# Layer 0's output projection in a two-layer streaming trunk: finished channels read back during the third head pair, and the value store in two parts

## The chip, the cores and the metric

The kernel runs on one core of a Trainium2 chip. The time is that of one execution on the device in microseconds, the median of the runs. Everything is kept feature-major: 128 features on the partitions, tokens along the columns. There are 1152 token columns, 1024 of a prompt and 8 x 16 of running streams, handled in three groups of 384 (G).

## The reference

Two layers, each a mixer and a squared-ReLU MLP with residuals and norms. The change is in the mixer of layer 0, which runs stick-breaking attention (8 heads of 64) beside a convolution module (512 channels, 31 taps), and joins both in one output projection:

```python
def ab_mixer_prompt(h, w_in, w_out, dw_w, dw_b, ln_g, ln_b):
    q, k, v, u = ab_project(h, w_in)             # u = a * sigmoid(g)
    ...
    a_out = a_out.reshape(B, T, SB_WIDTH)        # stick_breaking(q, k, v) over blocks of queries
    u_ext = jnp.pad(u, ((0, 0), (CONV_STATE, 0), (0, 0)))
    c_out = conv_module(u_ext, dw_w, dw_b, ln_g, ln_b)   # depthwise conv, layernorm, silu
    out = jnp.concatenate([a_out, c_out], axis=-1) @ w_out
    return out, k, v, u[:, T - CONV_STATE:]
```

The same is done for the running streams, whose keys and values come from a cache of 1024 positions. k and v are outputs too. The joined input of the projection has eight chunks of 128 features: chunks 0 to 3 are the attention's head pairs, chunks 4 to 7 the convolution's channels.

## The kernel before, in words

`mixer0` (L676) goes through four head pairs (`for p in range(4)`, L1004). Each large product is made of three passes over a high and a low part of the operands, so whatever TensorE multiplies with weights must first be split: ScalarE copies the high part (`split`, L186), VectorE subtracts it (L187). `put` issues a DMA from POOL's queue, `dma` one from SyncE's (SP in the profile). DMAs of either queue are issued in order, and an issue that has to wait holds what stands behind it.

**A pair.** `proj(p)` projects q, k and v of pair p in three groups of columns each; groups 0 and 1 are written by VectorE (L898), group 2 by ScalarE (L900). Once group 2 of k or v is there, POOL stores the whole tile (`sk`, `sv`) as an output (L902). `expand_qk` then splits q and k (L367, L369, L370, L372). `differences` (L914) replaces v in place by differences of neighbouring positions (L922 on VectorE, the first column L923 on ScalarE); since it overwrites `sv`, it has to wait until the store of L902 has read it. `expand_v` (L925) transposes the result (`vt`, L932). `attend` computes scores (`z`, L962, L963, L965), sigmoids (L966) and scans (L942, L947, L948), transposes the weights (`tpa`, L407), multiplies with the values (`ava`, L417) and sums the pieces (`cpa`, L431). Pairs 0 to 2 put their finished pieces in DRAM (`cat_d`, L382); pair 3 splits them straight into its place. The streams' attention (`zs`, `sgs`, `kps`; L589, L990 to L995) runs in between with cached keys (`ct03k`, loaded by SyncE, L558).

**The convolution.** Four channels groups c = 0 to 3 of 31 taps each (`tap`, L756) run on VectorE as filler: 26 taps beside the first projection, then 36, 38 and 24 in pairs 0, 1 and 2 (`TAPS`). The tiles `u` (input, two buffers, so channel 2 takes channel 0's place) and `y` lie in a pool `conv`. After the last tap POOL stores the result to `cat_d` (L759, L760).

**The last pair.** Pairs 0 to 2 have the next pair's projection as filler on TensorE; pair 3 has the output projection instead (`part_out`): for each output chunk of 128 features, sums over the read-back chunks 0 to 2 (`psoa`, L226). Its first three sums, over chunks 0 and 1 only, stand at its start (`first`). `ready_chunks` reads a chunk back from `cat_d` into the single buffer of the tag "sk" (`cr`, SyncE, L1100) and splits it into `cat0`. In the order of the work, chunks 0 and 1 are read back ahead of `first`, chunk 2 later (named "ready", 3 us of estimated work behind the last pieces of pair 2). `xo` (L1132) are the residual's rows, loaded by SyncE for each output chunk. Beside that, `conv_norm` (L1039) closes the pool `conv`, opens a pool `ln` in its place, loads the four channels of a column group (`yl`, L1053, POOL), takes the mean on TensorE (`mu`, L1059), centres (L1061), sums the squares (`ms_l`, L265), makes the reciprocal root on VectorE and ScalarE and broadcasts it by a product with diagonals (`rr_l`, L287).

**What sets the order.** `merge` interleaves lists of steps by an estimated TensorE time, respecting "after" and "lag"; `level` spreads the taps; the framework's scheduler then orders each engine's instructions, and each engine works through its own in order. The pool `early0` (`ep`) holds three buffers of the tag "sg" and two of "kp", which the streams' `kps` use (L987).

Of the kernel before, what the change touches and what calls it, by code (L numbers as in the profile page):

```python
# [8 lines left out]
F32 = mybir.dt.float32  # L9
# [6 lines left out]
P = 128  # L16
D = 1024
KC = 8
T = 1152
TP = 1024  # L20
TAPS = (26, 36, 38, 24)
G = 384
NG = 3
# [8 lines left out]
UW = UP + 8 * US  # L32
# [92 lines left out]
def tile_trunk(ctx, tc, ins, outs):  # L125
# [6 lines left out]
    put = nc.gpsimd.dma_start  # L132
# [43 lines left out]
    cat_d = [dram.tile([KC, P, T], F32, name=f"cat_d{l}") for l in range(2)]  # L176
# [7 lines left out]
    def split(hi, lo, src):  # L184

        ACT(hi, src, AF.Copy)  # L186
        return tt(lo, src, f(hi), ALU.subtract)  # L187
# [488 lines left out]
    def mixer0():  # L676
        with ExitStack() as st:

            ep = Bufs(st.enter_context(pool("early0")), sg=3, kp=2)
# [6 lines left out]
            pp = Bufs(st.enter_context(pool("pair0")), ve=2)  # L686
            wk = Bufs(st.enter_context(pool("work0")), wt=4, wts=1, cat=2)
            S = {"qb": qb}
# [15 lines left out]
            h, rstd = n0.h, n0.r  # L704


            us, ys, tapped = {}, {}, [0] * 4
            conv_pool = ExitStack()
            cv = Bufs(conv_pool.enter_context(pool("conv")), u=2, y=1)

# [30 lines left out]
            def tap(c, j):  # L741
                if j == 0:
                    ys[c] = cv.tile([P, T], F32, "y", f"y{c}")
                u, y = us[c], ys[c]
                wj = dw[:, c, j:j + 1]
                pairs = ((y[:, 0:TP], u[:, j:j + TP]),
                         (y[:, TP:].rearrange("p (b t) -> p b t", t=16),
                          u[:, UP:].rearrange("p (b t) -> p b t", t=US)[:, :, j:j + 16]))

                with tc.issue_after(prior["weights"].ins) if prior else ExitStack():  # L750
                    for dst, src in pairs:
                        if j == 0:
                            nc.vector.tensor_scalar(dst, src, wj, cvec[:, 0, c:c + 1], ALU.mult, ALU.add)
                        else:

                            stt(src if j == CW - 1 else dst, src, wj, dst, ALU.mult, ALU.add)  # L756
                tapped[c] += 1
                if j == CW - 1:
                    put(cat_d[0][4 + c, :, 0:TP], pairs[0][1])  # L759
                    put(cat_d[0][4 + c, :, TP:].rearrange("p (b t) -> p b t", t=16), pairs[1][1])  # L760
# [130 lines left out]
            def proj(p):  # L891
                steps = []
                for n, tag in enumerate(("sq", "sk", "sv")):
                    def evac(ps, g, n=n, tag=tag):
                        if g == 0:
                            S[tag, p] = pp.tile([P, T], F32, tag, f"{tag}0{p}")
                        if g < 2:
                            tt(S[tag, p][:, g * G:g * G + G], ps[:, :G], rstd[g], ALU.mult)  # L898
                        else:
                            ACT(S[tag, p][:, g * G:], ps[:, :G], AF.Copy)  # L900
                        if g == 2 and n:
                            put(outs["sb_k" if n == 1 else "sb_v"][p], S[tag, p])  # L902
                    steps += chunk_steps(at[4 * n + p], got, ahead, h, ks, evac, f"p{p}{n}")
                return steps

# [98 lines left out]
            for p in range(4):  # L1004
                S["p"] = p
                expand_qk(p)
                if p < 3:
                    fill = proj(p + 1)
                    if p < 2:
                        fill[10:10] = ag(p + 2)  # L1010
                    n = TAPS[p + 1]
                    mix, now, taps = [], taps[:n], taps[n:]
                else:
                    cat_t = new_hs("cat0")
                    (first, fill), now = part_out(0, range(3), pp, cat_t), []
                    for s in taps:
                        s.pe = 900.0
                    mix = taps + conv_norm(lambda: (conv_pool.close(), Bufs(st.enter_context(pool("ln")), t1=3, yl=5))[1],
                                           cat_t)
                cat = Cat(0, p, wk, cat_t)  # L1020
                jobs = attend(p, cat)
                body, left = pipeline(jobs[1:], jobs[0][2])
                steps = carry + [jobs[0][0]] + [Step(327.0, lambda p=p, g=g: expand_v(p, g)) for g in range(NG)]
                if p == 3:
                    late, = ready_chunks(0, [2], pp, cat_t)
                    late.name, late.after, late.lag = "ready", carry[-1].name, 3000.0
                    fill[0].after, fill[0].lag = "ready", 5000.0
                    fill = ready_chunks(0, range(2), pp, cat_t) + first + [late] + fill
                steps += [jobs[0][1]] + body
                carry = left  # L1030
                if p == 3:
                    steps += carry
                cs = sample_out(cat, wk, p)
                load = sample_caches(0, p, cp)
                sample = two_samples(*(sample_steps(0, p, bg, S, wk, load, soft, cs) for bg in range(2)))
                run(level(merge(steps, sample, fill, mix), now))
# [1175 lines left out]
```

## Time and profile before

| what | value |
|---|---|
| median of 3 runs | 2701.9 us (2701.33 to 2704.93) |
| the profiled execution's own time | 2699.14 us |
| its span | 2697.4 us |
| granted TensorE clock, mean | 0.995 |
| instructions | 42135 |
| HBM read, written | 299.56 MB, 122.58 MB |
| pair 0's value store issued | 104.85 us |
| the last pair's first read-back issued | 399.43 us |

The profile is of one execution; its times count from the start of the span. A row of the timeline has start, duration, engine, line, operation, output<-input, number of instructions, and in brackets how long the engine was idle before it and what released it. Tile names come without their numbers. PE is TensorE, PEld its weight loads, DVE VectorE, ACT ScalarE, POOL GpSimd, SPq SyncE's DMA queue.

### The profile page before, as it was taken

The page shows a single profiled execution, that of the slowest core. Times are in us where ns is not written, and L with a number is a line of the kernel's source. Part 1 is how long each engine was busy: PE and PEld are TensorE (multiplying, and loading weights), DVE is VectorE, ACT ScalarE, POOL GpSimd, SP SyncE. Part 2 cuts the span into 40 slices and gives each one's busy share as a digit, 9 for nine tenths or more (in the row PEclk, how much of TensorE's full clock was granted, in tenths as well). Part 3 has the DMA queues.
Part 4 walks back from the last instruction along what each step waited for, and adds up shares of the span by engine and source line. Part 5 has one row for each costly group of instructions (what it writes and reads, how often), then busy time and mean ns, then how long its engine had stood idle before and what let it go on. Part 6 is the DMA issues. An engine that isn't in the chain of part 4 may idle for free.

```text
span 2697.4 us, 42135 instructions
## 1 busy us (share of the span) xinstructions
PE 2643.2 (98%) x15404; PEld 2313.8 (86%) x15404; DVE 1989.0 (74%) x3820; ACT 1344.6 (50%) x2691; POOL 315.4 (12%) x535
## 2 busy tenths in 40 slices
PE   8999998999999999999999999999999999999998
PEld 8888886888888878888999999989988888888888
DVE  8999996896767654768577777778786767546677
ACT  6344456754444543445355555556554545433444
POOL 1100111131111100000011111110311111100001
PEclk9999999999999999999999999999999999999999
DMA  4344547534444497435444444446534444685344
GB/s 160 110 126 150 152 143 240 177 126 145 149 148 147 160 311 247 142 116 194 152 142 134 136 142 135 136 140 231 185 120 144 155 148 148 252 289 170 99 148 141
DMA packets 194095, 437.56 MB, mean 162 GB/s; under 512 B 26992, under 2 KB 71216, under 8 KB 191840
## 3 DMA queue, kind: packets, MB, share of 16 engines
q1 hardware_dynamic: 154320, 298.22, 33.9%
q0 software_dynamic: 39424, 136.64, 14.3%
q8 instruction: 121, 1.98, 0.3%
q14 instruction: 86, 0.70, 0.1%
q10 hardware_dynamic: 144, 0.02, 0.0%
HBM read 299.56 MB, written 122.58 MB: 156 GB/s over the span
## 4 chain that ended last, share of the span: by engine, by line
PE 83%; DVE 8%; issue 3%; ACT 3%; DMA 2%; POOL 0%; SPq 0%; DVEq 0%; ACTq 0%; POOLq 0%
PE um L1606 22%; PE psc L226 10%; PE psp L226 4%; PE usm L1618 3%; PE ps L1909 3%; PE psoa L226 2%; PE avc L488 2%; PE tpc L476 2%; PE f L226 1%; PE pd103None L1889 1%; PE pd100None L1889 1%; PE pd003None L1889 1%; PE pd000None L1889 1%; PE pd001None L1889 1%; PE pd101None L1889 1%
## 5 line engine op out<-in xcount | busy, mean ns | idle before, releaser
L226 PE MATMUL psc<-h,hl_wc 128*128 128x384 f32 x1728 | 328.8, 340 | 0.0
L226 PEld LDWEIGHTS psc<-h,hl_wc 128*128 128x128 f32 x1728 | 296.8, 188 | 9.2 <-issue 7.9
L1606 PE MATMUL um<-sl,hl_m 128*128 128x512 f32 x780 | 197.2, 393 | 0.0
L756 DVE SCALAR_TENSOR_TENSOR y<-u,dw,y 128x1024 f32<-128x1024 f32 (+1 forms) x232 | 177.7, 807 | 0.7
L1606 PEld LDWEIGHTS um<-sl,hl_m 128*128 128x128 f32 x780 | 145.1, 188 | 30.2
L226 PE MATMUL psp<-h,hl_wi 128*128 128x384 f32 x864 | 162.4, 340 | 0.0
L187 DVE TENSOR_TENSOR tm<-xr,tm 128x512 fp32r<-128x512 f32 (+1 forms) x120 | 78.6, 657 | 108.0 <-ACT tm L186 107.9
L226 PEld LDWEIGHTS psp<-h,hl_wi 128*128 128x128 f32 x864 | 148.3, 188 | 6.2 <-issue 5.1
L186 ACT ACTIVATE tm<-xr 128x512 fp32r<-128x512 f32 (+1 forms) x120 | 72.1, 600 | 118.7 <-PE pd103None L1889 21.3
L1230 ACT ACTIVATE s<-s,mxc 128x640 f32<-128x640 f32 (+4 forms) x128 | 88.8, 693 | 40.2 <-DVE mxc L1227 38.5
L186 ACT ACTIVATE whc<-tpc 128x512 fp32r<-128x512 f32 (+1 forms) x144 | 72.4, 524 | 63.7 <-PE tpc L476 60.4
L1227 DVE CUSTOM_DVE_ANT_0 s<-zc,bp 128x384 f32<-128x384 f32 (+3 forms) x128 | 66.1, 517 | 41.2 <-PE zc L1264 40.6
L1606 PE MATMUL um<-sl,hl 128*128 128x512 f32 x372 | 95.0, 395 | 0.0
L187 DVE TENSOR_TENSOR wlc<-tpc,whc 128x512 fp32r<-128x512 f32 (+1 forms) x144 | 83.2, 594 | 7.6 <-ACT whc L186 7.0
L1606 PEld LDWEIGHTS um<-sl,hl 128*128 128x128 f32 x372 | 70.0, 190 | 14.3
L1630 ACT ACTIVATE xr<-xr 128x512 f32<-128x512 f32 x64 | 40.4, 631 | 80.8 <-DVE xr L1629 80.8
L476 PE MATMUL tpc<-ident,s 128*128 128x128 f32 x480 | 73.6, 276 | 2.6 <-DVE s L1232 2.1
L187 DVE TENSOR_TENSOR xr<-xr,xr 128x512 fp32r<-128x512 f32 (+1 forms) x60 | 39.4, 656 | 46.9 <-ACT xr L186 46.9
L187 DVE TENSOR_TENSOR th<-xr,th 128x512 fp32r<-128x512 f32 (+1 forms) x62 | 40.8, 658 | 42.1 <-ACT th L186 42.1
L186 ACT ACTIVATE hl_m<-xr 128x512 fp32r<-128x512 f32 x54 | 34.1, 632 | 74.6 <-PE usm L1618 61.4
L186 ACT ACTIVATE th<-xr 128x512 fp32r<-128x512 f32 (+1 forms) x62 | 37.3, 601 | 66.4 <-PE pd003None L1889 13.1
L1263 PE MATMUL zc<-k,q 128*128 128x384 f32 (+1 forms) x192 | 66.2, 346 | 2.9 <-DVE cpc L498 2.9
(1050 smaller groups left out, 7166.4 us busy)
## 6 DMA issues: line engine op xcount, KB each, us to landing
xr<-hb_d SPq DMA_DIRECT2D x208, 256.0 KB, 2.8
xr<-in_w_up_dram SPq DMA_DIRECT2D x32, 512.0 KB, 3.7
rwm<-in_w_up_dram SPq DMA_DIRECT2D x32, 512.0 KB, 5.0
hb_d<-xr POOLq DMA_DIRECT2D x32, 512.0 KB, 3.4
hb_d<-t POOLq DMA_DIRECT2D x32, 512.0 KB, 3.2
wm<-in_w_down_dram SPq DMA_DIRECT2D x64, 256.0 KB, 3.4
st_wd<-in_w_down_dram SPq DMA_DIRECT2D x64, 256.0 KB, 3.5
st_wc<-in_w_in_c_dram SPq DMA_DIRECT2D x44, 256.0 KB, 2.9
```

The source lines that it names most:

```text
L186: ACT(hi, src, AF.Copy)
L187: return tt(lo, src, f(hi), ALU.subtract)
L226: mm(ps()[:, :G], hl[:, a, at:at + P], act[g][k // 4][b][:, k % 4, :], start=n == 0, stop=n == len(todo) - 1)
L476: nc.tensor.transpose(tp[:, c0 + q * P:c0 + (q + 1) * P], blocks.get(j, tile_q), ident)
L756: stt(src if j == CW - 1 else dst, src, wj, dst, ALU.mult, ALU.add)
L1227: nc.vector.tensor_tensor_reduce(s[:, c:c + m], z, b, -1.0, mx, ALU.add, ALU.min, new)
L1230: ACT(s[:, :n], s[:, :n], AF.Exp, bias=mx, scale=-1.0, accum_out=tot)
L1263: mm(z[:, :m], qs[i][:, qc], kd[i][:, kc], start=True, stop=False)
L1606: mm(banks[b, e], w[a][:, c], combo(key, c)[:, h], start=k < 3 and c == 0 and i == 0, stop=c == 3 and i == 2, skip_group_check=k > 2)
L1618: mm(samples[u][:, e * 256:e * 256 + 256], sample_combo(key, c)[h], w[a][:, c].rearrange("p e t -> p (e t)"), start=k == 0 and c == 0 and ...
L1889: mm(ps, w[:, a, m * P:m * P + P], b[:, h], start=first and s == 0, stop=j == NJ - 1 and s == 2, skip_group_check=k not in heads)
L1909: mm(rows[e], s[:, h], w[:, a], start=j == 0 and q == 0 and k != 0, stop=j == NJ - 1 and q == 2 and k != 3, skip_group_check=k in (3, 0))
```

## The change

Two things.

1. At tap 20 of channel 3, the 14th of the 24 taps in pair 2, POOL issues two reads: chunk 1 into a buffer `cr1` of the tag "kp" (a streams' buffer), and chunk 0 into `cr0` of the tag "u" (the place of channel 2, whose taps are over). The splits of both become six steps of their own at pair 3's start: four, then two steps carried over from pair 2, then the last two. `ready_chunks(0, range(2))` goes from the head of the filler; chunk 2 is read back as before.
2. The value store is split by columns: 0 to 767 once group 1 is written, 768 to 1151 once group 2 is. The store of k stays whole.

```diff
@@ mixer0
-            us, ys, tapped = {}, {}, [0] * 4
+            us, ys, tapped, crs = {}, {}, [0] * 4, {}
...
@@ tap(c, j)
                 tapped[c] += 1
+                if (c, j) == (3, 20):
+                    crs[0] = cv.tile([P, UW], F32, "u", "cr0")
+                    crs[1] = ep.tile([P, T], F32, "kp", "cr1")
+                    for n in (1, 0):
+                        put(crs[n][:, :T], cat_d[0][n])
                 if j == CW - 1:
...
@@ proj(p), evac
-                        if g == 2 and n:
-                            put(outs["sb_k" if n == 1 else "sb_v"][p], S[tag, p])
+                        if g == 2 and n == 1:
+                            put(outs["sb_k"][p], S[tag, p])
+                        if g and n == 2:
+                            own = slice(0, 2 * G) if g == 1 else slice(2 * G, T)
+                            put(outs["sb_v"][p][:, own], S[tag, p][:, own])
...
@@ the loop over pairs, p == 3
                     fill[0].after, fill[0].lag = "ready", 5000.0
-                    fill = ready_chunks(0, range(2), pp, cat_t) + first + [late] + fill
+                    fill = first + [late] + fill
+
+                    def come(c, g):
+                        hi, lo = (x[:, c, :] for x in cat_t[g][0])
+                        split(hi, lo, crs[c][:, g * G:g * G + G])
+
+                    backs = [Step(0.0, lambda c=c, g=g: come(c, g)) for g in range(NG) for c in range(2)]
+                    steps = backs[:4] + steps[:2] + backs[4:] + steps[2:]
                 steps += [jobs[0][1]] + body
```

The changed kernel's lines lie further down: L922 of before is L930 there, L962 is L970, L1061 is L1076, L1100 is L1115.

VectorE at the start of the first pair, before; sv00 is pair 0's value tile, y0 and u0 are channel 0's taps, sg000 the first query block's scan:

```order
L942 SCALAR_TENSOR_TENSOR sg000_1100<-sg000_1100,ones_74 128x128
L756 SCALAR_TENSOR_TENSOR y0_773<-u0_384,dw_77,y0_773 128x1024
L756 SCALAR_TENSOR_TENSOR y0_773<-u0_384,dw_77,y0_773 128x128
L756 SCALAR_TENSOR_TENSOR y0_773<-u0_384,dw_77,y0_773 128x1024
L922 TENSOR_TENSOR sv00_1005<-sv00_1005 128x1023
L756 SCALAR_TENSOR_TENSOR y0_773<-u0_384,dw_77,y0_773 128x1024
L898 TENSOR_TENSOR sq01_1181<-psp100_1107,rh0_317 128x384
```

The same place of the changed kernel:

```order
L950 SCALAR_TENSOR_TENSOR sg000_1101<-sg000_1101,ones_74 128x128
L756 SCALAR_TENSOR_TENSOR y0_773<-u0_384,dw_77,y0_773 128x1024
L930 TENSOR_TENSOR sv00_1005<-sv00_1005 128x1023
L756 SCALAR_TENSOR_TENSOR y0_773<-u0_384,dw_77,y0_773 128x1024
L756 SCALAR_TENSOR_TENSOR y0_773<-u0_384,dw_77,y0_773 128x128
L756 SCALAR_TENSOR_TENSOR y0_773<-u0_384,dw_77,y0_773 128x1024
L903 TENSOR_TENSOR sq01_1182<-psp100_1108,rh0_317 128x384
```

The differences have moved up past two tap instructions; one stands ahead of them instead of three.

VectorE at the start of the last pair, before; sg217 is the last scan of pair 2, cpa212 one of its sums, cat0_01 and cat0_11 are the low parts of chunks 0 and 1, hl_wo0a weights of the output projection:

```order
L948 TENSOR_TENSOR sg217_4254<-sg217_4254 128x511
L659 COPY cs02_4014<-sq021_4308 64x64
L187 TENSOR_TENSOR hl_wo0a2_0_4630<-st_wo0a2_0_4628,hl_wo0a2_0_4630 128x384
L187 TENSOR_TENSOR hl_wo0a3_0_4717<-st_wo0a3_0_4715,hl_wo0a3_0_4717 128x384
L431 TENSOR_TENSOR cpa212_4323<-ava212_4315,ata212_4322 64x256
L187 TENSOR_TENSOR cat0_01_4361<-cr00_4358,cat0_00_4360 128x384 x3
L922 TENSOR_TENSOR sv03_4093<-sv03_4093 128x1023
L187 TENSOR_TENSOR cat0_11_4378<-cr01_4375,cat0_10_4377 128x384 x3
```

The same place of the changed kernel:

```order
L956 TENSOR_TENSOR sg217_4262<-sg217_4262 128x511
L659 COPY cs02_4021<-sq021_4316 64x64
L187 TENSOR_TENSOR cat0_01_4353<-cr0_3955,cat0_00_4352 128x384
L187 TENSOR_TENSOR cat0_11_4357<-cr1_3956,cat0_10_4356 128x384
L431 TENSOR_TENSOR cpa212_4331<-ava212_4323,ata212_4330 64x256
L187 TENSOR_TENSOR cat0_01_4353<-cr0_3955,cat0_00_4352 128x384
L187 TENSOR_TENSOR cat0_11_4357<-cr1_3956,cat0_10_4356 128x384
```

The rows behind these are the last two splits, then the differences of sv03, then hl_wo0a2 and hl_wo0a3. On ScalarE the six splits stand ahead of the copies of k and q (L367, L369) and of sg217's sigmoids, where one weight split (hl_wo0a2) stood before; on SyncE chunk 0's and 1's reads are gone, and the read of chunk 2 has gone from just ahead of the second residual's rows (xo01) to just behind them. On POOL the read into cr0 stands ahead of pair 2's value store, the read into cr1 between the puts of cpa201 and cpa202.

TensorE ahead of chunk 2's first sums, before; psoa000 is output chunk 0 of column group 0, psoa011 output chunk 1 of group 1, cat0_20 the high part of chunk 2:

```order
L226 MATMUL psoa011_4644<-cat0_11_4378,hl_wo0a1_0_4392 128x384
L226 MATMUL psoa011_4644<-cat0_10_4377,hl_wo0a1_0_4392 128x384
L417 MATMUL ava300_4654<-wa3000_4599,vs0_749 64x256
L417 MATMUL ava300_4654<-wa3000_4599,vs0_749 64x128
L962 MATMUL z3040_4667<-k0_745,q0_743 128x512
L226 MATMUL psoa000_4402<-cat0_20_4541,hl_wo0a0_0_4387 128x384
L226 MATMUL psoa010_4633<-cat0_20_4541,hl_wo0a1_0_4392 128x384
```

The same place of the changed kernel; rr_l0 is the layer norm's broadcast of group 0, z3030 the fourth query block's scores:

```order
L973 MATMUL z3030_4606<-maskd_128,unit_129 128x128
L589 MATMUL zs0310_4591<-ct03k11_4512,qb0_126 32x256 x4
L287 MATMUL rr_l0_4613<-sq_l00_4532,ones_74 128x384
L226 MATMUL psoa010_4640<-cat0_00_4352,hl_wo0a1_0_4371 128x384
L226 MATMUL psoa000_4395<-cat0_20_4566,hl_wo0a0_0_4366 128x384
L226 MATMUL psoa010_4640<-cat0_01_4353,hl_wo0a1_0_4371 128x384
L226 MATMUL psoa001_4420<-cat0_20_4566,hl_wo0a0_0_4366 128x384
```

Before, the twelve sums of psoa010 and psoa011 over chunks 0 and 1 ran between the scores z3030 and chunk 2's first sum, and rr_l0 came behind chunk 2's sums; now rr_l0 comes directly behind z3030, with chunk 2's sums mixed into psoa010's.

## The prediction

> **What bounds the kernel now.** I read the page first, then the waits of TensorE, then the stretches around its two longest waits in the first mixer, by windows and by the timeline.
>
> ```profile
> PE 2643.2 (98%) x15404; PEld 2313.8 (86%) x15404; DVE 1989.0 (74%) x3820; ACT 1344.6 (50%) x2691; POOL 315.4 (12%) x535
> ```
>
> TensorE is busy for 2643.2 of the span's 2697.4 us. The change adds and removes no matmul, so it can win only part of the 54 us of idle time, or time lost to a lowered clock. The waits say whose idle time the change touches:
>
> ```profile
> PE psoa L226 <- ACT cat L186: 5.9, 2, 5.3
> PE vt L932 <- ACT sv L923: 2.9, 1, 2.9
> PE tpa L407 <- DVE sg L948: 2.2, 2, 1.3
> ```
>
> The first row is the output projection waiting for the split of a read-back chunk, at the start of the last pair; the second is the first pair's transposes waiting for the value differences. These are the change's two targets: 8.8 us. The third lies just ahead of the first and isn't touched.
>
> **First pair, the value store in two parts.** Windows first (window; busy time of PE, PEld, DVE, ACT, POOL; granted clock; DMA share), then the timeline of POOL, DVE and PE, then the landing of the store:
>
> ```profile
> 108.00:110.00 2.00, 0.56 (x4) 0.24 (x2) 2.00 (x4) 0.00 (x0) 0.00 (x0) 1.00 0.56 211
> 110.00:112.00 2.00, 0.57 (x5) 0.60 (x6) 2.00 (x2) 0.21 (x2) 0.00 (x0) 1.00 0.00 0
> 112.00:114.00 2.00, 2.00 (x16) 1.08 (x15) 1.91 (x3) 1.31 (x4) 0.00 (x0) 0.68 0.00 0
> 114.00:116.00 2.00, 2.00 (x13) 1.07 (x12) 1.20 (x3) 0.96 (x3) 0.00 (x0) 0.50 0.62 206
> ```
>
> ```profile
> 104.85 0.55 POOL L902 DMA_DIRECT2D out_sb_v_dram<-sv  x1 [3.93 <-ACT sv L900]
> 107.20 2.72 DVE L756 SCALAR_TENSOR_TENSOR y<-u,dw,y 128x1024 f32<-128x1024 f32 x3
> 109.83 1.22 DVE L922 TENSOR_TENSOR sv<-sv 128x1023 f32<-128x1023 f32 x1
> 111.43 1.18 PE L932 MATMUL vt<-ident,sv 128*128 128x128 f32 x9 [2.87 <-ACT sv L923]
> ```
>
> ```profile
> DMA to landing us min/median/max: 3.9/3.9/3.9
> ```
>
> The store of 576 KB is issued at 104.85 and has landed at 108.75; the differences overwrite its source, so they could start then. They start at 109.83, because three taps stand ahead of them on VectorE. In the new order one tap of 1024 columns stands ahead, two go behind. A group of three with one small tap takes 2.72 us, so a large one takes about 1.2: the new place is reached at 108.4. The second part, 192 KB, is issued when the whole was; it lands between the 3.4 us of a 64 KB put (quoted below) and the 3.9 us of the whole, so at 108.3 to 108.75. The differences then start at about 108.5, 1.3 us earlier, and TensorE's wait falls from 2.87 to about 1.55 us. Bounds: nothing (if the second part, queued behind the first, lands 1.1 us later than the whole did) and 1.4 (a start at 108.4). I take 1.3, since the new landing lies between two rows that are close together.
>
> Behind the wait the granted clock is 0.68 and then 0.50: with 1.00 and 0.50 as the two rates, 0.68 means that the half rate began at 112.7, and TensorE worked some 3.3 us at half rate, which cost 1.65 us. A wait of 1.3 us just ahead of the last pair (the third row of the waits) left the clock at 1.00 (window 404 below); 1.55 is nearer to that than to 2.87, so I count three quarters of 1.65: 1.2 us. Term of the first pair: 2.5 us, between 0 and 1.4 + 1.65 = 3.1.
>
> The Trainium skill, "TensorE: Matmul & The Clock Gate", section "What's actually happening", lets the clock fall after at least one idle window of about 3.4 us. By that no drop could follow a wait of 2.87 us, the clock part of this term would be nothing, and the term 1.3. The trace disagrees: 0.50 stands behind the 2.87.
>
> In pairs 1 and 2 TensorE waits for no differences, so the split store is worth nothing there; four more POOL issues of 0.55 us each vanish in an engine that is 12% busy.
>
> **Last pair, the early read-back.** The same views, with the DMA queue of SyncE (SPq):
>
> ```profile
> 404.00:406.00 2.00, 0.00 (x0) 0.00 (x0) 0.41 (x1) 0.37 (x1) 1.30 (x3) 1.00 1.03 392
> 406.00:408.00 2.00, 0.00 (x0) 0.00 (x0) 0.00 (x0) 0.00 (x0) 1.00 (x3) 0.56 1.01 401
> 408.00:410.00 2.00, 0.97 (x4) 0.90 (x5) 0.99 (x3) 1.35 (x3) 1.48 (x3) 0.50 1.08 401
> 410.00:412.00 2.00, 2.00 (x12) 1.55 (x14) 1.64 (x3) 0.71 (x2) 0.02 (x1) 0.50 1.16 252
> 412.00:414.00 2.00, 2.00 (x19) 0.76 (x11) 0.00 (x0) 0.47 (x2) 0.00 (x0) 0.73 1.03 412
> ```
>
> ```profile
> 399.43 0.34 SPq L1100 DMA_DIRECT2D cr<-cat_d  x1
> 410.53 0.33 SPq L1100 DMA_DIRECT2D cr<-cat_d  x1
> ```
>
> ```profile
> 408.45 1.35 ACT L186 ACTIVATE cat<-cr 128x384 fp32r<-128x384 f32 x3 [4.09 <-DMA cr<-cat_d]
> ```
>
> ```profile
> 409.03 0.69 PE L226 MATMUL psoa<-cat,hl_wo0a 128*128 128x384 f32 x1 [5.35 <-ACT cat L186]
> 417.58 2.80 PE L226 MATMUL psoa<-cat,hl_wo0a 128*128 128x384 f32 x12 [0.51 <-ACT cat L186]
> 422.75 0.33 PE L962 MATMUL z<-k,q 128*128 128x128 f32 x1
> ```
>
> Chunk 0's read takes from 399.43 to 408.45, 9.0 us beside a DMA share of 1.0; chunk 1's can only start at 410.53, when the single buffer is split. With both in the memory since the third pair, the two waits of 5.35 and 0.51 us go: 5.9. So does the half rate: it runs from inside window 406 to inside window 412 (0.73 means 1.1 us of it), over 0.97 + 2.00 + 1.1 = 4.1 us of TensorE work; at full rate that is 2.0 us less. The first score of the pair, at 422.75, comes 7.9 us earlier if nothing else is late.
>
> What can be late next are the layer norm's loads, which go ahead of that score in TensorE's order and are issued by POOL once chunk 0's read-back place, part of the closed pool, has been split:
>
> ```profile
> 405.78 0.58 POOL L1053 DMA_DIRECT2D yl<-cat_d  x1
> 407.36 1.60 POOL L1053 DMA_DIRECT2D yl<-cat_d  x3 [1.00 <-DMA cat_d<-u]
> ```
>
> ```profile
> DMA to landing us min/median/max: 6.3/6.8/7.1
> ```
>
> The first of these loads waits in POOL's queue, with the other three behind it. In VectorE's new order the splits stand around the sum cpa212, and ScalarE has done its half of them long before:
>
> ```profile
> 403.99 0.42 DVE L431 TENSOR_TENSOR cpa<-ava,ata 64x256 f32<-64x256 f32 x1
> ```
>
> Four or five splits, at some 0.5 us each, fall ahead of chunk 0's end, two of them ahead of that sum, where VectorE had copies and weight splits before that move back: an end at about 405.7, so that the loads are issued about as now. The last of the first four lands at 409.0 + 6.8 = 415.8 by the old landing, and from 412 on if they gain from the two reads of 576 KB that no longer run beside them (3 us at the 400 GB/s of window 406). By the order TensorE has 18 sums, transposes and scores ahead of the norm's mean, some 8 us from 403.5. I take no loss, because the crowd that made 6.8 us is what goes; the bound is some 2.5 us lost (415.8 against 411.5, less what of the mean runs on the earlier loads).
>
> The six splits cost ScalarE 2.7 us (twice 1.35), now ahead of the last pair's q and k. One weight split of 0.53 moves out of there, and a gap takes more:
>
> ```profile
> 395.07 0.53 ACT L186 ACTIVATE hl_wo0a<-st_wo0a 128x384 fp32r<-128x384 f32 x1 [1.39 <-PE psp L226]
> 397.80 1.09 ACT L966 ACTIVATE sg<-z 128x512 f32<-128x512 f32 x2
> ```
>
> ```profile
> 400.69 1.22 DVE L947 TENSOR_TENSOR_SCAN sg<-sg 128x512 f32<-128x512 f32 x1
> ```
>
> 2.7 less 1.39 and 0.53 is 0.8 us later; the scan that needs these sigmoids starts 1.8 us behind their end, so this is covered. With that cover gone it would cost up to 0.8.
>
> **What is given back.** In the new order the norm's broadcast rr_l0 and the sums of chunk 2 stand ahead of twelve sums of the second output chunk that ran in between before:
>
> ```profile
> 425.90 0.73 PE L265 MATMUL ms_l<-ones,sq_l 128*128 128x1 f32 x6
> 427.93 0.64 PE L589 MATMUL zs<-ct03k,qb 128*32 128x256 f32 x8 [1.30 <-ACT qb L580]
> 432.84 3.25 PE L226 MATMUL psoa<-cat,hl_wo0a 128*128 128x384 f32 x15
> ```
>
> ```profile
> 431.95 0.68 DVE L283 TENSOR_SCALAR sq_l<-ident,v_l 128x128 f32<-128x128 f32 x3
> ```
>
> From the norm's mean (425.90) to the diagonals that rr_l0 multiplies (432.63) took 6.7 us on ScalarE and VectorE. Between the two, TensorE now has the wait of 1.30, two groups of zs (0.64 each), and seven matmuls of transposes and scores at 0.22 (3.25 us for 15): 4.1. A new wait of 2.6 us is left. It is about as long as the 2.87 of the first pair, so I add an even chance of a half-rate stretch of up to 1.65 us, and with it a rounded 0.7. Bounds: 0 (VectorE, less crowded, gets the rows done sooner) and 3.9 + 1.65 (the wait of 1.30 goes, and this one grows by as much).
>
> Behind it the sums wait for chunk 2's own read, which SyncE now issues behind the next residual's:
>
> ```profile
> 427.70 1.43 SPq L1132 DMA_DIRECT2D xo<-in_x_dram  x1
> ```
>
> ```profile
> 423.75 3.44 DMA cat_d<-cpa
> 427.25 4.99 DMA cr<-cat_d
> ```
>
> Its source is stored about 8 us earlier too, so its 1.4 us behind xo costs little: I count 0, with 1.5 as the bound. So of 7.9 us, 7.9 − 2.6 − 0.7 = 4.6 are kept, between 1 and 7.9.
>
> ```profile
> 433.00:525.00 92.00, 88.74 (x647) 72.88 (x648) 71.89 (x154) 68.23 (x146) 8.14 (x15) 1.00 0.53 178
> ```
>
> The rest of the mixer is TensorE's by 88.74 of 92 us, so what is kept here is kept to the end; its 3.3 us of idle time may move by 1.5 either way.
>
> Sum: 2.5 + 4.6 = 7.1 us. From the profiled execution's 2699.14 us that gives 2692.0; it was 2.8 us under the median of the runs shown, so from 2701.9 the forecast is **2694.8**.
>
> **The rivals.** *Given back.* The norm's loads bind TensorE (2.5 us), or the new wait grows and drops the clock (to 5.6), or the first pair's clock falls all the same (1.2): any two of these leave 2 to 4 us of gain, 2698 to 2700. For it: DMA share 1.0 in all five windows around 404 to 414. Against it: two reads of 576 KB are gone from there. In the Trainium skill, "SBUF — State Buffer", section "🔬 SBUF: two separate sides", a transfer issued by GpSimd has its descriptors held up while VectorE runs an operation in a two-port mode. That would push the norm's loads back, and speaks for this rival; it does not show here for the additions and taps of this kernel: the store of 104.85 landed at 108.75 inside a stretch in which VectorE was busy for 2.00 of 2.00 us.
>
> *Clean.* No new wait at rr_l0, because the chain of 6.7 us held queueing on VectorE that goes: 2.5 + 7.9 = 10.4, 2691.5. For it: some of that chain was VectorE at other rows. Against it: its two table loads and the scans stay.
>
> *Nothing moves.* The scheduler's new order of the last pair loses elsewhere what it wins, or the splits are held back, so that the projection waits as before: 2700 to 2704. Against it: the order shows the splits ahead of q and k.
>
> *Slower.* One mechanism: ScalarE and VectorE process in order, and the six splits stand ahead of the last pair's q and k, the sigmoids of 397.80 and the value's eviction. If chunk 1's read lands after about 395, everything behind stands still, and TensorE runs dry within some 6 us. It is issued between two puts of POOL with this gap between them:
>
> ```profile
> 349.36 0.53 POOL L382 DMA_DIRECT2D cat_d<-cpa  x1 [15.12 <-DVE cpa L431]
> ```
>
> So it starts some 45 us ahead; the longest read-back took 9.0. It would have to be held for 36 us more, for its buffer or its source, and from 20 us beyond that on it makes the kernel 7 to 13 us slower: 2709 to 2715.
>
> **How the numbers follow.** About 0.2%, 5.4 us, can be told from no change: faster is below 2696.5, slower above 2707.3. My forecast (2692.5 to 2697.5) gets 0.45, given back 0.22, clean 0.15, nothing moves 0.10, slower 0.08. Faster: 0.39 of the first, all of clean and 0.03 of given back, 0.57. Slower: 0.08 and a trace of nothing moves, 0.09. The same: 0.34. The range 2689.5 to 2702.0 leaves out slower, half of nothing moves and the far end of clean.
>
> **What would show it.** Right: transposes of the first value wait about 1.5 us at a clock of 1.00; no psoa wait for cat at the start of the last pair, no half rate there, first score 7.9 and 2.5 us earlier, near 412.4; a new wait at rr_l0 near 2.6. Wrong: a wait for yl at mu, the clock at 0.50 behind the first pair's wait, cr1 landing after the third pair, or the mixer's end not moving with the first score.

## The result and the profile after

| kernel | median, us | executions | ratio to before, 95% interval |
|---|---|---|---|
| before | 2700.31 | 11 | |
| changed | 2694.56 | 11 | 0.9981 [0.9973, 0.9988] |
| changed, run again (run 5) | 2694.01 (before there: 2700.09) | 12 | 0.9976 [0.9965, 0.9987] |

The medians lie 5.7 us apart; by the first ratio the change makes the kernel 5.1 us faster, with 3.2 to 7.3 us in its interval. One execution of run 9 fell into a slow state (5014.56 us at a granted clock of 0.889) and is left out of its median and its ratio below. The profiled execution took 2694.56 us with a span of 2692.8.

The waits of TensorE in the changed kernel: the row for psoa waiting for a split (5.9 us) is gone, vt's wait has halved, and two rows are new, mu (the norm's mean) waiting for its loads and rr_l (the norm's broadcast) waiting for the diagonals.

```profile
PE mu L1074 <- DMA yl<-cat_d: 2.8, 3, 2.3
PE tpa L407 <- DVE sg L956: 2.0, 2, 1.0
PE rr_l L287 <- DVE sq_l L283: 1.6, 1, 1.6
PE psoa L226 <- ACT wa L409: 1.4, 1, 1.4
PE vt L940 <- ACT sv L931: 1.4, 1, 1.4
```

The first pair, in the timeline of VectorE, POOL and TensorE, and in two windows (PE, PEld, DVE, ACT, POOL busy, clock, DMA share, GB/s):

```profile
106.10 0.55 POOL L910 DMA_DIRECT2D out_sb_v_dram<-sv  x1 [2.09 <-ACT sv L905]
108.46 1.26 DVE L756 SCALAR_TENSOR_TENSOR y<-u,dw,y 128x1024 f32<-128x1024 f32 x1
109.64 1.22 DVE L930 TENSOR_TENSOR sv<-sv 128x1023 f32<-128x1023 f32 x1
111.24 1.17 PE L940 MATMUL vt<-ident,sv 128*128 128x128 f32 x9 [1.42 <-ACT sv L931]
```

```profile
112.00:114.00 2.00, 2.00 (x24) 0.93 (x22) 2.00 (x5) 1.50 (x5) 0.00 (x0) 1.00 0.00 0
114.00:116.00 2.00, 2.00 (x16) 2.00 (x13) 2.00 (x3) 1.47 (x3) 0.00 (x0) 1.00 0.98 287
```

The differences start as soon as the one tap ahead of them is done; the wait is 1.42 us and the clock behind it 1.00, where it was 0.68 and 0.50. The place as a whole comes 1.25 us later than in before's profile (the store is issued at 106.10 against 104.85); this execution has a half-rate stretch at 50 us that the other lacks. So the waits are to be compared, not the times.

The last pair, TensorE's timeline:

```profile
400.99 0.55 PE L407 MATMUL tpa<-ident,sg 128*128 128x128 f32 x3 [1.02 <-DVE sg L956]
401.30 1.68 PE L226 MATMUL psoa<-cat,hl_wo0a 128*128 128x384 f32 x6
408.10 1.56 PE L1074 MATMUL mu<-yl,ones 128*128 128x384 f32 x4 [0.34 <-DMA yl<-cat_d]
411.95 1.65 PE L1074 MATMUL mu<-yl,ones 128*128 128x384 f32 x2 [2.29 <-DMA yl<-cat_d]
419.35 0.33 PE L970 MATMUL z<-k,q 128*128 128x128 f32 x1
429.28 1.65 PE L287 MATMUL rr_l<-sq_l,ones 128*128 128x384 f32 x2 [1.64 <-DVE sq_l L283]
430.16 6.18 PE L226 MATMUL psoa<-cat,hl_wo0a 128*128 128x384 f32 x27
521.44 10.69 PE L226 MATMUL psob<-cat,hl_wo0b 128*128 128x384 f32 x60 [0.58 <-ACT cat L186]
```

```profile
412.00:416.00 4.00, 3.82 (x12) 1.16 (x12) 0.54 (x2) 0.00 (x0) 0.00 (x0) 0.50 0.38 141
424.00:428.00 4.00, 3.12 (x22) 1.40 (x22) 3.90 (x6) 3.62 (x6) 0.00 (x0) 0.69 1.00 341
428.00:432.00 4.00, 2.72 (x6) 2.12 (x7) 3.55 (x11) 2.44 (x5) 0.00 (x0) 0.50 0.67 221
```

The projection's first sums run without a wait at 401.30. Then the mean waits for three of its four loads, 2.29 us for the third, and the half rate begins at the end of that wait (411.8). It comes again from 425.5 to 432.3. That is ahead of the wait at rr_l, which begins at 427.64, so the wait can't have started it.

A reader who compares just these two profiles would be misled about the place of the gain. The mixer ends with the sums of psob, and at their last long row the changed kernel is not ahead:

```profile
520.96 10.70 PE L226 MATMUL psob<-cat,hl_wo0b 128*128 128x384 f32 x60 [0.58 <-ACT cat L186]
2689.66 0.58 PE L265 MATMUL ms_fin<-ones,accfin 128*128 128x1 f32 x4 [1.17 <-DVE accfin L2013]
```

```profile
2684.91 0.58 PE L265 MATMUL ms_fin<-ones,accfin 128*128 128x1 f32 x4 [1.16 <-DVE accfin L2028]
```

The first fence is of before, the second of the changed kernel. At psob it is 521.44 against 520.96, 0.5 us behind; at the end it is 4.8 us ahead. The rest of the program, which the change doesn't touch, took 5.2 us less in this one execution, and before's profile has four half-rate stretches there (near 597, 1812, 1843 and 1979 us) of which this one has none: some 13.7 us at half rate, up to 6.8 us of time. In the last pair it is the other way round. From the transposes ahead of the projection's first sums to the first sum of psob, before took 112.2 us with 6.8 us of half rate in it, this profile 114.4 with 17.1, and a second profile of the same kernel (run 5) 109.1 with 3.4. Which part of the change pays can therefore not be read from one profile of each; the runs below measure it.

### The profile page after: what moved, and what is told of

It is laid out like the page before. It is cut to its first block, busy times and chain, and to the rows that moved or that the text cites. A ratio compares the mean times of both kernels' runs of the same rounds, so it can differ in the third digit from the quotient of the medians.

```text
span 2692.8 us, 42134 instructions
## 1 busy us (share of the span) xinstructions
PE 2644.0 (98%) x15404; PEld 2311.8 (86%) x15404; DVE 1990.0 (74%) x3820; ACT 1343.9 (50%) x2691; POOL 318.2 (12%) x541
## 4 chain that ended last, share of the span: by engine, by line
PE 83%; DVE 9%; issue 3%; ACT 3%; DMA 2%; POOL 0%; SPq 0%; DVEq 0%; ACTq 0%; POOLq 0%
PE um L1621 22%; PE psc L226 10%; PE psp L226 4%; PE usm L1633 3%; PE ps L1924 3%; PE psoa L226 2%; PE avc L488 2%; PE tpc L476 2%; PE f L226 1%; PE pd100None L1904 1%; PE pd000None L1904 1%; PE pd102None L1904 1%; PE pd002None L1904 1%; PE pd101None L1904 1%; PE pd001None L1904 1%
## 5 line engine op out<-in xcount | busy, mean ns | idle before, releaser
L1621 PE MATMUL um<-b11m,hl_m 128*128 128x512 f32 x288 | 68.1, 391 | 0.0
```

What stands on the lines that cost most here:

```text
L1621: mm(banks[b, e], w[a][:, c], combo(key, c)[:, h], start=k < 3 and c == 0 and i == 0, stop=c == 3 and i == 2, skip_group_check=k > 2)
```

## The experiments

Each ratio is to the kernel before, timed on the same chip. The medians of before there were 2701.46 us (runs 1 to 4), 2700.09 (5 to 8) and 2700.03 (9 to 11).

### 1 and 2. One half of the change each

Run 1 is before with the two-part value store alone:

```diff
-                        if g == 2 and n:
-                            put(outs["sb_k" if n == 1 else "sb_v"][p], S[tag, p])
+                        if g == 2 and n == 1:
+                            put(outs["sb_k"][p], S[tag, p])
+                        if g and n == 2:
+                            own = slice(0, 2 * G) if g == 1 else slice(2 * G, T)
+                            put(outs["sb_v"][p][:, own], S[tag, p][:, own])
```

> The kernel before with the value store in two parts alone; chunks 0 and 1 are read back as before. Theory (both halves of the change pay, each about half): the first pair's transposes wait 1.4 us instead of 2.9, mostly with no half-rate stretch behind it, 2.5 to 3.0 us faster than before (ratio 0.9989 to 0.9991); the last pair's psoa waits of 5.4 and 0.5 stay. Rival 1 (the store carries the whole gain, the read-back gives all of its own back): 5 to 6 us faster (0.998). Rival 2 (the gain measured is the luck of the clock's windows): within 1 us of before.

Run 2 is the changed kernel with this edit taken back, so that only the early read-back is left.

> The changed kernel with the value store in one piece again; only the early read-back is left. Theory (each about half): 2.5 to 3.5 us faster than before (0.9987 to 0.9991); the wait of 2.9 at the first pair is back, the psoa waits of the last pair stay away, and in their place stand waits for yl at mu (2 to 3 us) and for the diagonals at rr_l (1.5 to 2.5 us). Rival 1 (the store carries the gain): within 1 us of before. Rival 2 (luck of the clock's windows): within 1 us of before too, told apart by the first run.

Run 1: 2696.50 us, 0.9988 [0.9979, 0.9997]. Run 2: 2696.53 us, 0.9987 [0.9977, 0.9997]. Each half is worth 3.2 to 3.5 us by the ratios (the theory said 2.5 to 3.0 and 2.5 to 3.5). The intervals are wide, but neither reaches 1, so it is unlikely that either half gives all of its own back, or that the luck of the clock is the cause. In run 1's profile the psoa waits, expected to stay at 5.4 and 0.5, are 6.4 (chunk 0) and 0.9 (chunk 2). TensorE comes to the transposes ahead of the first sum 0.9 us earlier than in before (401.79 against 402.70), and the sum starts no earlier (409.12 against 409.03), so part of what the store wins is waited for at the next late transfer. Rival 1's 0.998 lies at the edge of run 1's interval; it needs run 2 to be level with before, and that run lies 3.5 us below. TensorE's waits in run 2:

```profile
PE mu L1071 <- DMA yl<-cat_d: 3.8, 3, 2.1
PE vt L937 <- ACT sv L928: 2.9, 1, 2.9
```

The first pair's wait is back, and the norm's loads are late (3.8 us over the three column groups).

### 3. The mean behind the first scores

```diff
-                     Step(2600.0, centre, 1900.0, f"c{name}", f"l{name}", 4000), Step(500.0, squares, 1400.0),
+                     Step(2600.0, centre, 1900.0, f"c{name}", f"l{name}", 12000 if g == 0 else 4000), Step(500.0, squares, 1400.0),
```

> The changed kernel with the first column group's mean put later in the order of the work (its lag 12000 instead of 4000), so that TensorE has the scores of the first three query blocks ahead of it, and the broadcast rr_l0 behind the second output chunk's sums. Theory (the early read-back is given back by the wait for the norm's loads, by the wait at rr_l0 and by half-rate stretches behind both): both waits go, 2.8 + 1.6 us and up to 1.65 us for each of two stretches, so 3 to 6 us faster than the changed kernel (2689 to 2692). Rival (the norm's chain of loads, mean, squares and rows sets the pace of the last pair): its later start is paid in full further on, no gain or 1 to 3 us slower than the changed kernel.

2697.27 us, 0.9986 [0.9977, 0.9995]: not faster than the changed kernel. The waits at mu and at rr_l are gone from the first group, and another has come, in TensorE's and SyncE's timeline:

```profile
424.04 1.10 PE L226 MATMUL psoa<-cat,hl_wo0a 128*128 128x384 f32 x2 [3.87 <-ACT cat L186]
```

```profile
419.58 0.34 SPq L1115 DMA_DIRECT2D cr<-cat_d  x1
```

The sums of chunk 2 came up on TensorE before its read-back, issued at 419.58, had landed and been split. The streams' scores also wait 1.38 us for their cached keys there, at 409.65. So the theory falls as it was put. The rival's number (no gain, or 1 to 3 us slower than the changed kernel) came true, but not its reason, the norm's chain: what was late next was the third read-back. Filling one wait with work from further on only brings TensorE sooner to the next transfer.

### 4 and 9. The broadcast later

```diff
-                     Step(800.0, lambda: box["rows"](), 0.0, None, f"s{name}", 2500)]
+                     Step(800.0, lambda: box["rows"](), 0.0, None, f"s{name}", 5000 if g == 0 else 2500)]
```

> The changed kernel with only the broadcast rr_l0 put later (lag 5000 instead of 2500): it stands behind the second output chunk's sums again, as before the change; the mean stays where it is. Theory (the wait of 1.6 us at rr_l0 and a half-rate stretch around it are given back there): 1.5 to 3.5 us faster than the changed kernel (2691 to 2693). Rival (the sums behind it wait for chunk 2's read-back anyway): no difference to the changed kernel within 1 us.

> The fourth run's kernel (rr_l0 later) once more, on one chip with the next two. Theory (a wait at rr_l0 and, in some executions, a half-rate stretch at that place are all that it saves): ratio to before 0.997 again. Rival (the fourth run was a lucky set of executions): 0.998, as the changed kernel.

2692.33 us, 0.9970 [0.9959, 0.9981], and once more 2692.38 us, 0.9967 [0.9954, 0.9980]. The wait at rr_l is gone, and no other has come in its place:

```profile
PE mu L1074 <- DMA yl<-cat_d: 2.6, 4, 1.3
PE tpa L407 <- DVE sg L956: 2.0, 2, 1.0
PE psoa L226 <- ACT wa L409: 1.4, 1, 1.4
PE vt L940 <- ACT sv L931: 1.4, 1, 1.4
PE zs L589 <- ACT qb L580: 1.3, 1, 1.3
```

About 2 us of the read-back's gain had been lost at this place. That figure is less certain than the others: the intervals overlap those of the changed kernel, which was not timed beside them, and only both runs together (12 executions, mean 2692.4 us, against 23 with 2694.8) set the two apart. The half-rate stretch near 424 us stayed, in both profiles of this kernel (424.5 and 422.5), so the wait at rr_l does not make it. It begins 1.2 to 1.5 us after a wait of 1.30 us, that of the scores zs for qb.

### 5. The changed kernel again

No edit.

> The changed kernel once more, unedited, for a second profile and for its times beside the next ones on one chip. Theory (a wait of 1.5 us or more drops the clock for one stretch of 3.4 us in some executions and not in others, by where a free-running window of the clock falls, so that executions differ by some 1.7 us for each such stretch): the same waits at vt, mu and rr_l as in the first profile within 0.5 us each, but half-rate stretches at other places and in another number; ratio 0.998 again. Rival (the stretches belong to fixed places of the program): the same stretches at the same places.

2694.01 us, 0.9976 [0.9965, 0.9987]. The waits at vt (1.42), mu (2.9 in sum) and rr_l (1.25) are those of the first profile, and the half-rate stretches are elsewhere: none behind the mean, one near 421, and then at 591, 1806, 1837, 1977 and 2653 us. The first score of the pair comes at 415.19, 15.1 us after the transposes that end pair 2's scans; in the first profile it was 18.4, and 20.1 in before. The rival, the same stretches at the same places, falls, while the waits are fixed. The theory's threshold falls too: the stretch at 421 follows a wait of 1.30 us, not 1.5 or more. But the places are not free either: over all thirteen profiles the same few come back, one between 590 and 600 us in ten, one between 1833 and 1846 in eight. The last section shows why.

### 6 and 10. Chunk 0's splits first

```diff
-                    backs = [Step(0.0, lambda c=c, g=g: come(c, g)) for g in range(NG) for c in range(2)]
+                    backs = [Step(0.0, lambda c=c, g=g: come(c, g)) for c in range(2) for g in range(NG)]
```

with the edit of run 4.

> The changed kernel with the broadcast rr_l0 later (as in the fourth run) and the six splits in another order, chunk 0's three first, so that its place is free three splits earlier on VectorE and POOL can issue the norm's loads earlier. Theory (the mean waits for loads that are issued late, behind the last split of chunk 0): the loads are issued 1.0 to 1.5 us earlier, the waits at mu fall from 2.6 to 1.0 to 1.6 us, and with fewer half-rate stretches it is 1 to 3 us faster than the fourth run (ratio 0.996 to 0.997). Rival (they land late because the transfers of residual rows and cached keys share the engines): the loads land no earlier, no difference to the fourth run (0.997).

> The sixth run's kernel (rr_l0 later, chunk 0's splits first) once more. Its waits at mu were no shorter than without the new order of the splits (2.4 against 2.6 us), so if only waits and half-rate stretches make the time, it is the same as the kernel beside it within 1.5 us (0.9965 to 0.9972). If the order of the splits itself pays, 2 us or more faster than the kernel beside it (0.996 or less).

2689.81 us, 0.9956 [0.9942, 0.9970], and once more 2691.85 us, 0.9960 [0.9944, 0.9975]; run 9 beside it took 2692.38. POOL's timeline of run 6 tells why the waits at mu hardly moved (2.4 us against 2.6):

```profile
402.09 0.56 POOL L1068 DMA_DIRECT2D yl<-cat_d  x1
404.36 1.07 POOL L1068 DMA_DIRECT2D yl<-cat_d  x2 [1.70 <-DMA cat_d<-u]
405.80 1.08 POOL L1068 DMA_DIRECT2D yl<-cat_d  x2 [0.38 <-issue]
```

The first load is issued 1.0 us earlier than in run 4, as expected, but the second now waits 1.70 us for the store of the last convolution channel to land (`cat_d<-u`), whose place it takes, and the others stand behind it on POOL. The same release stands already in before's row at 407.36, which the prediction quotes (1.00 us for `cat_d<-u`). Neither of my two reasons was the whole: not the last split alone, and not only crowded engines, but one more release right behind the first. The theory's number for run 6 (0.996 to 0.997) nearly came true, its mechanism, shorter waits at mu, did not. Side by side this order is 0.5 us faster by the medians, too little to tell from none, though the ratio of 0.9960 is the one expected if the order itself pays; that it is the fastest in both of its runs I can't put down to a cause. Against the changed kernel on the same chip, run 6 is 4.2 us faster (run 5 took 2694.01); the intervals of their ratios just overlap.

### 7 and 11. The mean a little later

Run 7 is the edit of run 3 with 9000 in place of 12000; run 11 is run 6 with 7000.

> The changed kernel with the first column group's mean a little later in the order (lag 9000): behind the streams' scores and pair 2's last products, still ahead of the new pair's scores; rr_l0 then comes far later. Theory (the waits at mu and rr_l can both be filled without holding up chunk 2's sums, which were late in the third run): 2 to 4 us faster than the changed kernel (ratio 0.9965 to 0.9975). Rival (whatever is put later, the next late transfer or split takes the wait): no faster than the changed kernel (0.998).

> The kernel of the run beside it with the mean's lag at 7000 in place of 4000: two groups of the streams' scores (1.1 us of TensorE work) fall ahead of and between the mean's products, where TensorE waited for the norm's loads. Theory (the waits at mu can be filled): the waits at mu and behind them fall by 1 us or more, 0.5 to 1.5 us faster than the kernel beside it. Rival (the streams' scores there wait for their cached keys instead, as in the third run): no difference, or slower, with a wait for ct03k in place of one for yl.

Run 7: 2692.08 us, 0.9968 [0.9956, 0.9980], as the theory said, though run 5's interval on the same chip overlaps it, so the rival isn't excluded; the waits at mu and rr_l of the first group are gone, and its one large new wait is 2.3 us at the sum of the squares. Run 11: 2692.19 us, 0.9967 [0.9954, 0.9979], no faster than run 10. In its timeline the time saved at mu is lost again at the cached keys and at chunk 2:

```profile
423.80 0.64 PE L589 MATMUL zs<-ct03k,qb 128*32 128x256 f32 x8 [0.67 <-DMA ct03k<-in_sb_k_dram]
427.42 2.97 PE L226 MATMUL psoa<-cat,hl_wo0a 128*128 128x384 f32 x15 [1.52 <-ACT cat L186]
```

The rival holds there.

### 8. The early reads from SyncE

```diff
-                        put(crs[n][:, :T], cat_d[0][n])
+                        dma(crs[n][:, :T], cat_d[0][n])
```

> The changed kernel with the two early reads issued by SyncE instead of POOL, at the same place of the program. Theory (the reads start more than 35 us ahead of their splits, so who issues them costs nothing): the same as the changed kernel within 1 us (0.998), landing within 6 us in both. Rival (GpSimd's issue is held up beside VectorE's work, or the reads hold POOL's puts up): 1 to 3 us faster than the changed kernel, with reads that land sooner than the 4 to 6 us of POOL's. Rival on the other side (the reads hold SyncE's weight and cache loads up): slower than the changed kernel, with waits for weights in the third pair.

2695.42 us, 0.9975 [0.9965, 0.9985], level with run 5 beside it. The two reads landed 7 us after their issue, not within the 6 us expected, and not sooner than POOL's:

```profile
L762 SPq DMA_DIRECT2D cr<-cat_d x2: 327/328/330, 302.0 to 353.8; - x2
DMA to landing us min/median/max: 6.9/7.0/7.0
```

Who issues them costs nothing that these executions show, and no wait for weights came into the third pair.

## Why the prediction was right, and where its steps failed

**The first pair: right, a little small.** The wait was forecast at 1.55 us; it is 1.41 to 1.43 in each of the eleven profiles with the split store, without a half-rate stretch behind it in any of them. The parts landed 2.6 to 2.7 us after their issue in the changed kernel's first profile, sooner than my bounds of 3.4 to 3.9, which changes nothing, since the tap ahead decides. The forecast of 2.5 us stands against 3.2 by run 1's ratio, inside its interval. The clock's part was rightly put as a chance: the 2.87 us that dropped the clock in before's profile left it at 1.00 in run 2's.

**The psoa waits: right.** For chunks 0 and 1 they are gone in every kernel with the early read-back. The reads landed within 6 us in the profile and were issued more than 35 us ahead of their splits, so the rival on the slower side had nothing to stand on; run 8 shows that POOL's queue has no part in it either.

**The step that failed: "I take no loss, because the crowd that made 6.8 us is what goes".** The two reads went, but the DMA engines stayed busy, and TensorE came sooner. The norm's loads in the changed kernel, and the window in which the mean waits for them:

```profile
404.53 1.67 POOL L1068 DMA_DIRECT2D yl<-cat_d  x3 [0.99 <-DVE cat L187]
406.58 1.08 POOL L1068 DMA_DIRECT2D yl<-cat_d  x2 [0.38 <-issue]
```

```profile
408.00:412.00 4.00, 1.61 (x5) 0.72 (x5) 0.09 (x1) 0.36 (x1) 0.00 (x0) 0.98 1.00 344
```

```profile
DMA to landing us min/median/max: 3.5/6.2/7.3
```

They are issued as forecast (404.5, within half a microsecond of 405.8 less the 1.7 us that all of it is earlier) and land after 6.2 us in the median, 7.3 at most; the DMA share is still 1.00. TensorE is there at 407.8, 2 us earlier than the 411.5 I allowed less the same 1.7. So the first group's mean waits 2.8 us in the first profile, 2.4 in the second and 1.6 in run 8's. Counted from the transposes ahead of it, the first score is 1.7 us earlier in the first profile and 4.9 in the second, not 7.9. The shortfall adds up: of the 6.2 us missing in the first profile 2.8 are the waits and up to 3.4 the half-rate stretch of 6.8 us behind them, of the 3.0 us missing in the second 2.4 are the waits. What was put at nothing cost more than the bound of 2.5 us in one of two profiles. It is the first mechanism of the rival "given back", and the prediction's own sign of being wrong, a wait for yl at mu, did appear.

**What is given back: right in kind.** The new wait at rr_l was forecast at 2.6 us and measured 1.0 to 1.9. (The row at 425.90 from which the chain was counted is the sum of the squares, ms_l, not the mean; the count of 6.7 us is that of the rest of the chain, as it should be.) A half-rate stretch, an even chance in the sum, is there in both profiles of the changed kernel, but it begins ahead of this wait (425.5 against 427.6, and 420.8 against 423.9), so that part came out right by luck. Chunk 2's read behind the residual's cost no wait, as forecast. The rest of the mixer kept its idle time within the 1.5 us allowed, though a half-rate stretch near 486 us fell into it in the first profile.

**The sum.** The 7.9 was too much, by the mean's waits and what followed them; the 2.6 + 0.7 was about right in size. The read-back's net was forecast at 4.6 us; by run 2 it is 3.5 [0.8 to 6.2], and by run 1 set against both halves together 2 to 3. So the store was a little too small and the read-back too large, and the total, 7.1 against 5.1 to 6.5 by the two ratios, came out close; that the forecast's 2694.8 met the median of 2694.56 is luck in part: the gain was put some 1.4 us too large against the medians' 5.7, and before's median is 1.6 us lower over eleven executions than over the first three. The read-back alone keeps the most uncertain number here: the stretches of single executions are as large as what it is worth.

## What to carry to other kernels

When the wait that ends last is a transfer, list the transfers queued behind it and ask when each is issued and what releases its place: here three in a row (the norm's loads, the last channel's store, chunk 2's read-back) stood close behind each other, and each made the next wait, of 1.7 to 3.9 us, as soon as the one ahead was gone. A small wait that the new order makes is often cheaper to remove than the large one that it replaced: putting one broadcast later, a number in a table, was worth about another 2 us, and this version, with or without chunk 0's splits first, takes 2690 to 2693 us. And where executions of one program differ by as much as the edit is worth, time the halves of the edit apart; two profiles side by side put the gain in the wrong part of the program. The stretches of half rate came only where TensorE was idle for more than a third of 3.4 us, and those are few places: a wait that is gone takes its chance of a stretch with it.

## What the runs showed of the hardware

**The clock's stretches come by chance.** The executions of the changed kernel differ in the mean granted clock, and the time goes with it: four at 0.997 took 2689.5 to 2693.4 us, three at 0.995 took 2694.6 to 2696.1, two at 0.994 took 2698.5 and 2699.1. In windows of 1 us over thirteen profiles, every half-rate stretch that the program's end doesn't cut is 3.4 or 6.8 us long. The same wait brings one or doesn't. In before's profile the wait of 2.87 us in the first pair was followed by one; here is run 2, behind the same wait:

```profile
112.27 1.17 PE L937 MATMUL vt<-ident,sv 128*128 128x128 f32 x9 [2.87 <-ACT sv L928]
```

```profile
107.87:111.29 3.42, 1.52 (x9) 1.20 (x7) 3.42 (x5) 0.00 (x0) 0.00 (x0) 1.00 0.59 220
111.29:114.70 3.41, 2.43 (x28) 1.69 (x28) 3.41 (x4) 1.68 (x6) 0.00 (x0) 1.00 0.00 0
114.00:116.00 2.00, 2.00 (x19) 1.51 (x18) 1.79 (x4) 1.39 (x4) 0.00 (x0) 1.00 0.36 110
```

Run 5, behind a wait of 1.30 us:

```profile
420.36 0.70 PE L589 MATMUL zs<-ct03k,qb 128*32 128x256 f32 x8 [1.30 <-ACT qb L580]
```

```profile
417.39:420.80 3.41, 2.11 (x23) 1.75 (x21) 2.40 (x5) 3.28 (x11) 0.00 (x0) 1.00 0.80 241
420.00:422.00 2.00, 1.64 (x12) 1.16 (x13) 1.97 (x3) 1.79 (x5) 0.00 (x0) 0.70 0.97 333
422.00:424.00 2.00, 1.87 (x11) 0.56 (x10) 1.90 (x5) 1.55 (x2) 0.00 (x0) 0.50 0.92 322
```

The first left the clock at 1.00, the second was followed by 0.70 and 0.50. The Trainium skill, "TensorE: Matmul & The Clock Gate", section "What's actually happening", has windows of about 3.4 us; the length of every stretch agrees. It also wants an idle window of that length ahead of a drop, and there the runs differ: 1.30 us of waiting was enough here, with TensorE at work for 2.11 of the 3.41 us ahead of the drop. Nor does the order of the two waits fit a threshold on the wait alone.

**Where the windows lie.** The beginnings of the stretches show it. Within each of the thirteen profiles the distance between any two of them is a whole multiple of 3.4133 us, to within 0.03 us. In run 5 they begin at 420.80, 591.46, 1806.62, 1837.34, 1977.28 and 2653.12 us: the later ones 50, 406, 415, 456 and 654 windows after the first (2232.32 us for 654). So one grid of windows runs through each execution from beginning to end. It lies differently in each, which is the luck: a wait can fall into one window or across two. In before the wait from 108.56 to 111.43 lies mostly in this window:

```profile
109.30:112.70 3.40, 1.27 (x13) 1.12 (x17) 3.40 (x5) 0.91 (x3) 0.00 (x0) 1.00 0.00 0
```

TensorE was busy for 1.27 of its 3.40 us, and the half rate began at its end, 112.70. In run 2 the grid cuts the same wait at 111.29, TensorE was busy for 1.52 and 2.43 us of the two windows shown above, and the clock stayed. Between the first 6 us and 2690 us, over all thirteen profiles, every such window at full clock in which TensorE was busy for less than 0.44 of the time was followed by half rate, and none with more than 0.63; in between both occurred (the window ahead of run 5's stretch, 2.11 of 3.41, is one of the busiest). So busy time decides in the main, but not alone; what else counts, and what makes a stretch last one window or two, stays open.

**POOL's transfers beside a busy VectorE.** The two early reads of run 5, POOL's timeline, the window of the first, and the landing of both:

```profile
302.69 0.57 POOL L762 DMA_DIRECT2D cr<-cat_d  x1
354.77 0.56 POOL L762 DMA_DIRECT2D cr<-cat_d  x1
```

```profile
303.00:309.00 6.00, 6.00 (x44) 5.64 (x46) 6.00 (x9) 1.95 (x5) 0.26 (x1) 1.00 0.69 193
```

```profile
DMA to landing us min/median/max: 5.3/5.5/5.8
```

VectorE was busy for 6.00 of 6.00 us, and the reads landed in 5.3 to 5.8, against 7 from SyncE's queue in run 8. The hold-up of GpSimd's descriptors that the Trainium skill states ("SBUF — State Buffer", section "🔬 SBUF: two separate sides") for VectorE's two-port modes does not show beside the taps, scans and other two-input operations that VectorE ran in this window. No run here shows that any of them runs in such a mode, so this is no test of the rule.
